# HGRN2 score matmuls reordered by shape over the chunks, and the meta state padded to 128 rows

## Chip, cores and metric

One core of a Trainium2 chip runs the whole program. The metric is the device time of one execution in microseconds (us); the median of three timed runs stands for the kernel before. The engines are named as in the profile: PE is TensorE (matmuls), PEld its weight loads, DVE VectorE, ACT ScalarE, POOL GpSimd, SP the engine that only issues DMAs here.

## The reference, cut to what matters

A decoder block reads 512 tokens with 16 learned meta tokens ahead of them. It mixes tokens with forgetting attention and with an HGRN2 recurrence, and ends in a mixture of experts. The change touches the recurrence, which for 8 heads (key and value width 128) computes, chunk by chunk:

```
b = cumsum(log_f); o_inter = (q * exp(b)) @ state
scores[t, s] = sum_k q[t, k] * k[s, k] * exp(b[t, k] - b[s, k])   for s <= t
o = o_inter + scores @ v
new_state = exp(b_last) * state + (k * exp(b_last - b)).T @ v
```

The first chunk is the 16 meta tokens; it only provides the first state.

## The kernel before

The program has two halves. In the first, a list of projections (`proj`, line 344 through `mm3`) runs on PE: 128-column tiles of the input weights, each split by ACT (line 158) and DVE (line 159, `cut`) into a high and a low part, are multiplied with the normalised input. Beside them `stage` holds a generator per HGRN head (`hgrn`) and per attention pair (`attend`); after every three matmuls of a projection `stage.step()` lets the generator issue its next piece, so the pieces of a head stand between the projections of the next head in PE's order. A scheduler of the language orders the instructions of these engines; SP's DMAs are in the order of the code. In the second half 201 MB of expert weights (`w_e`, tile `ch`) stream in while PE multiplies them (lines 1126 and 1166). Tiles of the stream live in slots that the first half's tiles give free.

`hgrn` takes the 512 tokens of a head as 4 chunks of 128. The score matrix of a chunk is built from squares below the diagonal, each from factors that are referred to the middle of the square (`levels`): one 64x64 square (`l64`, called the far pair), two 32x32 squares (`l32`), and in the four 32x32 diagonal blocks one matmul of 32 columns (`kys`, `qys`) and three of 16 columns (`l4`, `l8`, `l16`). All contract over 128 rows. Far pairs and `l32` squares go to the PSUM tile `pc` (view `p4`), the diagonal blocks to `pd` (view `d4`). The output rows of a matmul are the PSUM partitions that it writes, and so its column group of the array: 64 wide for the far pair, 32 wide for all others. In the code that the diff shows, the loop over chunks `c` is outermost and the four matmuls of a diagonal block stand together.

DVE then masks `pd` into `sD` (lines 564 and 566), ACT copies `pc` into the score tile `sT` (lines 569 to 571), and the diagonal blocks follow (lines 575 and 577). Four steps after the score matmuls PE multiplies the scores with the values (tile `po`, lines 582 and 583).

The meta state: `pm` holds the transposed values and keys of the 16 meta tokens, line 510 copies them to `mt_`, a tile of 16 partitions, and line 519 multiplies them over 16 rows into `pi`, ahead of the three state updates of line 521, which contract over 128 rows.

In the early part, lines 222 to 225 (`fa`) project the forget gates: 8 matmuls per token block with 32 output rows each, the inner loop over the four column groups.

Of the kernel before, what the change touches and what calls it, by code (L numbers as in the profile page):

```python
# [13 lines left out]
AF = mybir.ActivationFunctionType  # L14
# [4 lines left out]
M = 16  # L19
# [4 lines left out]
NB = S // 128  # L24
# [40 lines left out]
def hybrid_block(tc, I, out, dbg=None):  # L65
    nc = tc.nc
    V, A, G, T = nc.vector, nc.scalar, nc.gpsimd, nc.tensor
    ctx = ExitStack()
    with ctx:
# [8 lines left out]
        def slot(name, n=4, dt=F32, w=None, stream=False):  # L78

            t_ = sb.tile([128, SLOT], dt, tag="stream" if stream else "slot", bufs=STREAM if stream else SLOTS, name=name)  # L80
            w = w or {4: L, 2: 1024, 1: 2048}[n]
            return t_[:, :n * w].rearrange("p (n w) -> p n w", n=n)
# [5 lines left out]
        def bank(name, main=False):  # L88
            return ps.tile([128, 512], F32, tag="main" if main else "side", bufs=4, name=name)
# [11 lines left out]
        ca, cc = slot("ca", 1)[:, 0], slot("cc", 1)[:, 0]  # L101
        used = {}

        def inside(c, n, dt=F32):

            o = used.get(id(c), 0)
            used[id(c)] = o + n
            return c[:, o:o + n].bitcast(dt)
# [306 lines left out]
            V.memset(sT[i], 0.0)  # L415
            V.memset(sD[i], 0.0)

        mt_ = inside(cc, 256)[:M]

        LEV = (64, 32, 16, 8, 4)  # L420

# [34 lines left out]
        def hgrn(h, f, b, q, v, g, kd, qe):  # L456
# [5 lines left out]
            def by(ap, w):  # L462
                return ap.rearrange("p (c t) -> p c t", t=w)
# [42 lines left out]
            pm = bank("pm")  # L506
            T.transpose(pm[:M, 0:128], v[:, 0:M], ident)
            T.transpose(pm[:M, 128:256], kd[:, 0:M], ident)
            mt = mt_[:, 0:256]
            V.tensor_copy(mt, pm[:M, :256])  # L510
            A.activation(eb[:, 3], br, AF.Exp)
            for _ in range(2):
                yield
# [21 lines left out]
            for j, w in enumerate(LEV):  # L535
                e = by(lev[j], 2 * w)
# [11 lines left out]
            p4, d4 = by(pc, 128), by(pd, 128)  # L548
            l64, l32, l16, l8, l4 = lev
            for c in range(NB):  # L550
                o = 128 * c
                T.matmul(p4[0:64, c, 64:128], l64[:, o:o + 64], l64[:, o + 64:o + 128], start=True, stop=True)
                for j in range(2):
                    r = slice(64 * j, 64 * j + 32)
                    T.matmul(p4[r, c, 64 * j + 32:64 * j + 64], l32[:, o + 64 * j:o + 64 * j + 32],
                             l32[:, o + 64 * j + 32:o + 64 * j + 64], start=True, stop=True)
                for j in range(4):
                    r, o = slice(32 * j, 32 * j + 32), 128 * c + 32 * j
                    T.matmul(d4[r, c, 0:32], kys[:, o:o + 32], qys[:, o:o + 32], start=True, stop=True)
                    for z_, (l, w) in enumerate(((l4, 4), (l8, 8), (l16, 16))):  # L560
                        T.matmul(d4[r, c, 32 + 16 * z_:48 + 16 * z_], l[:, o:o + 32],  # L561
                                 by(l[:, o:o + 32], 2 * w)[:, :, w:], start=True, stop=True)
            sc, sd = sT[h % 2], sD[h % 2]
            V.copy_predicated(sd, m4c, d4[:, :, 0:32])
            for z_, w in enumerate((4, 8, 16)):
                V.copy_predicated(sd.rearrange("p c (a t) -> p c a t", t=2 * w)[:, :, :, w:],
                                  mx_[w].rearrange("p c (a t) -> p c a t", t=w),
                                  d4[:, :, 32 + 16 * z_:48 + 16 * z_].rearrange("p c (a t) -> p c a t", t=w))
            A.activation(sc[0:64, :, 64:128], p4[0:64, :, 64:128], AF.Copy)
            A.activation(sc[0:32, :, 32:64], p4[0:32, :, 32:64], AF.Copy)  # L570
            A.activation(sc[64:96, :, 96:128], p4[64:96, :, 96:128], AF.Copy)
            for j in range(4):
                r = slice(32 * j, 32 * j + 32)
# [28 lines left out]
        for h in range(8):  # L602
            pf = proj(True)
            f, v, b, kd = (piece(n_, keep=n_ in "fv") for n_ in ("f", "v", "b", "kd"))
            q, g, qe = (piece(n_, F32, S) for n_ in ("q", "g", "qe"))
            logistic(f, pf, True)
            pi = proj(True)
            if h == 0:
                m4c, mx_ = within()
            both(lambda o, i_: A.activation(o, i_, AF.Copy), v, pi)  # L610
            V.tensor_scalar(f, f, lb[:, 1, h:h + 1], lb[:, 0, h:h + 1], op0=ALU.mult, op1=ALU.add)
            A.activation(b, f, AF.Ln)
            V.tensor_tensor_scan(b, reset, b, 0.0, op0=ALU.mult, op1=ALU.add)
            V.tensor_scalar(f, f, -1.0, 1.0, op0=ALU.mult, op1=ALU.add)
            pq = proj(False)
            A.activation(q, pq, AF.Copy, scale=128 ** -0.5)
            pg = proj(False)
            logistic(g, [pg], later=True)
            stage.add(hgrn(h, f, b, q, v, g, kd, qe))
# [10 lines left out]
        for d in range(KD):  # L630
            wh, wl = weights()
            p = bank("py", True)
# [6 lines left out]
        def attend(pr, X, Y, v):  # L639
# [7 lines left out]
            yield  # L647
            pm = bank("pm")
            T.transpose(pm[:M, 0:128], v[:, 0:M], ident)
            vm = mt_[:, 128 * (pr % 2):128 * (pr % 2) + 128]  # L650
            V.tensor_copy(vm, pm[:M, :128])
            yield
            hd = [slice(64 * h, 64 * h + 64) for h in range(2)]
# [18 lines left out]
            for i in range(NB):  # L672
                P = M + 128 * i
                r = slice(128 * i, 128 * i + 128)
# [35 lines left out]
            for c in range(NB):  # L710
                for h in range(2):
                    T.matmul(po[hd[h], 128 * c:], vt[:, c, hd[h]], pt_[h][:, 512 * c:384 * c + 512],  # L712
                             start=(c == 0), stop=(c == NB - 1))
# [8 lines left out]
        for pr in range(4):  # L722
            pk = proj(True)

            Y = slot("Y", 4, F32R)
            X = [[piece(f"X{h}{j}", F32R, S) for j in range(2)] for h in range(2)]
            for h in range(2):
                r = slice(64 * h, 64 * h + 64)
                nc.gpsimd.dma_start(Y[64:66, 2 * h + 1], chl[2 * pr + h:2 * pr + h + 1])
                V.tensor_scalar(X[h][1][64:66], mhalf[64:66, 0:1].to_broadcast([2, S]), 2.0, None, op0=ALU.mult)  # L730
                both(lambda o, i_: A.activation(o, i_[r], AF.Copy), Y[0:64, 2 * h], pk)
                for i in range(2):
                    o = slice(264 * i, 264 * i + 264)
                    V.tensor_tensor(Y[0:64, 2 * h + 1, o], pk[i][r], Y[0:64, 2 * h, o].bitcast(F32), op=ALU.subtract)
                G.tensor_copy(Y[64:128, 2 * h], Y[0:64, 2 * h].bitcast(F32))
            pq = proj(False)
            for h in range(2):
                r = slice(64 * h, 64 * h + 64)
                A.activation(X[h][0][0:64], pq[r], AF.Copy, scale=0.125)
                V.scalar_tensor_tensor(X[h][0][64:128], pq[r], 0.125, X[h][0][0:64].bitcast(F32), op0=ALU.mult, op1=ALU.subtract)  # L740
                G.tensor_copy(X[h][1][0:64], X[h][0][0:64].bitcast(F32))
            pv_ = proj(True)
            v_ = piece("v")
            both(lambda o, i_: A.activation(o, i_, AF.Copy), v_, pv_)
            stage.add(attend(pr, X, Y, v_))
# [11 lines left out]
        for d in range(KD):  # L757
            wh, wl = weights()
            p = bank("py", True)
            mm3([p], wh, wl, lambda k, i: oaT_h[:, k], lambda k, i: oaT_l[:, k], 4)  # L760
            g, t = ga[d], mix[d // 4][:, d % 4]
# [491 lines left out]
        with tc.If(nc.values_load(extrai[0:1, 32:33], min_val=0, max_val=16) > 0):  # L1253
# [4 lines left out]
            for half in range(2):  # L1258
                with tc.For_i(0, 16) as p:
# [4 lines left out]
                    with tc.For_i(0, nb):  # L1264
# [19 lines left out]
                        for k in range(KD):  # L1284
                            w = slot("wx", 2)[:, 0]
                            nc.sync.dma_start(w, I["w_e"][bass.ds(12 * p + k, 1), :, 1024 * half:1024 * half + 1024]
                                              .rearrange("o p c -> (o p) c"))
                            for n in range(2):
                                T.matmul(ph[n], xT[k // 4][:, k % 4], w[:, 512 * n:512 * n + 512],
                                         start=(k == 0), stop=(k == KD - 1))  # L1290
# [7 lines left out]
                        for n in range(2):  # L1298
                            for k in range(4):
                                w = slot("wx", 2)[:, 0, :512]  # L1300
                                c = 1024 * (k % 2) + 512 * half
# [4 lines left out]
                        for n in range(2):  # L1306
                            A.activation(yh, py[n], AF.Copy)
                            V.tensor_tensor(yl, py[n], yh.bitcast(F32), op=ALU.subtract)
                            c = slice(512 * n, 512 * n + 512)
# [66 lines left out]
```

## Time and profile before

| | |
|---|---|
| timed runs | 1098.28 us median of 3 (1097.28 to 1099.87) |
| the profiled execution | 1096.76 us, of which its span is 1094.8 us |
| busy in the span | PE 1047.2 us (96%), PEld 689.2, DVE 575.0 (53%), ACT 329.5 (30%), POOL 67.7 |
| mean granted clock of PE | 0.993 |
| w_e stream | 189 transfers of 1024 KB, DMA engines at 420 GB/s from about 700 us on |

The profile covers one execution. The span is from its first to its last instruction; a row of the timeline begins with the start in us from the span's start and the duration in us. A matmul in fp32 is one instruction of the program and two records each of weight load and matmul in the trace; records overlap, so that the distance of starts, not the duration, tells what one costs. Idle time in brackets is that of the engine before the row, and what ended it.

### The profile page before, as it was taken

The numbers are of one execution on the slowest core, as the hardware profiler recorded it, in microseconds if no ns is written. First come the engines' busy times: TensorE is split into PE (matmuls) and PEld (weight loads), VectorE is DVE, ScalarE is ACT, GpSimd is POOL, SyncE is SP. The second block draws the span as 40 slices with busy tenths as digits, with TensorE's granted clock in tenths as the row PEclk, the third lists the DMA queues.
The fourth block names the chain that finished last, engine by engine and source line by source line (L and its number), as shares of the span: only waits on it lengthen the run. The fifth ranks groups of instructions, "written<-read, shape, count | busy, mean of one in ns | idle before, by whom it ended". The sixth has DMA issues, their size and how long they took to land.

```text
span 1094.8 us, 16543 instructions
## 1 busy us (share of the span) xinstructions
PE 1047.2 (96%) x6756; PEld 689.2 (63%) x6757; DVE 575.0 (53%) x1269; ACT 329.5 (30%) x643; POOL 67.7 (6%) x88
## 2 busy tenths in 40 slices
PE   9999999999999999999999999999999999988984
PEld 8888988988888898777788634333443333333331
DVE  6967877677633466666653533333443333323324
ACT  5545655555551243344434300000000000000003
POOL 5000000000000121100000000000000000000002
PEclk9999999999999999999999999999999999999997
DMA  6211221121222211221287999999999999999993
GB/s 221 95 44 74 78 78 43 75 79 40 78 86 89 96 59 59 79 77 39 77 323 299 321 419 419 418 419 420 419 418 420 419 419 420 420 420 418 420 415 127
DMA packets 41139, 255.61 MB, mean 233 GB/s; under 512 B 6143, under 2 KB 6399, under 8 KB 12000
## 3 DMA queue, kind: packets, MB, share of 16 engines
q1 hardware_dynamic: 37328, 248.39, 57.3%
q0 software_dynamic: 2416, 3.98, 1.0%
q10 hardware_dynamic: 1312, 2.11, 0.5%
q8 instruction: 55, 0.90, 0.3%
q14 instruction: 28, 0.23, 0.1%
HBM read 254.15 MB, written 4.19 MB: 236 GB/s over the span
## 4 chain that ended last, share of the span: by engine, by line
PE 60%; DMA 32%; DVE 4%; issue 1%; ACT 1%; POOL 0%; DVEq 0%; SPq 0%; ACTq 0%; POOLq 0%
DMA ch<-w_e 30%; PE pj L344 24%; PE py L344 6%; PE pk L344 5%; PE phu L1126 4%; PE pye L1166 4%; PE pd L561 1%; PE ph L1026 1%; PE pu L215 1%; PE ph L1024 1%; PE poa L712 1%; PE ph L1025 1%; PE pout L1212 1%; DMA xslot<-rows_of,xslot 1%; DMA rows_of<-v 1%
## 5 line engine op out<-in xcount | busy, mean ns | idle before, releaser
L344 PE MATMUL pj<-uh,ws 128*128 128x512 f32 (+1 forms) x928 | 295.0, 363 | 1.6 <-DVE ws L159 1.1
L1126 PE MATMUL phu<-ch,xslot 128*64 128x512 f32 x1024 | 232.6, 598 | 20.7 <-DMA ch<-w_e 20.7
L344 PEld LDWEIGHTS pj<-uh,ws 128*128 128x128 f32 x928 | 174.8, 189 | 27.3 <-issue 2.0
L1126 PEld LDWEIGHTS phu<-ch,xslot 128*64 128x64 f32 x1024 | 68.1, 136 | 175.9 <-issue 113.0
L344 PE MATMUL pj<-ul,ws 128*128 128x512 f32 (+1 forms) x464 | 164.1, 354 | 0.0
L1139 DVE TENSOR_TENSOR hs<-hs,phu 128x512 f32<-128x512 f32 x16 | 11.0, 688 | 208.6 <-PE phu L1126 191.4
L159 DVE TENSOR_TENSOR ws<-w,ws 128x1024 fp32r<-128x1024 f32 (+1 forms) x84 | 98.0, 1168 | 34.3 <-ACT ws L158 34.1
L1166 PE MATMUL pye<-ch,hs 128*64 128x512 f32 x512 | 113.9, 596 | 1.6 <-DVE hs L1152 1.1
L158 ACT ACTIVATE ws<-w 128x1024 fp32r<-128x1024 f32 (+1 forms) x83 | 84.2, 1015 | 54.0 <-PE py L344 40.3
L344 PE MATMUL pk<-uh,ws 128*128 128x264 f32 x352 | 95.4, 285 | 0.0
L344 PEld LDWEIGHTS pj<-ul,ws 128*128 128x128 f32 x464 | 87.4, 188 | 9.5 <-issue 0.2
L1214 DVE SCALAR_TENSOR_TENSOR x<-pout,gate,x 128x512 f32<-128x512 f32 x128 | 87.1, 742 | 1.1 <-PE pout L1213 1.1
L1138 ACT ACTIVATE hs<-phu 128x512 f32<-128x512 f32 x16 | 9.6, 597 | 254.6 <-PE phu L1126 254.6
L1166 PEld LDWEIGHTS pye<-ch,hs 128*64 128x64 f32 x512 | 35.1, 137 | 71.5 <-issue 64.6
L1170 ACT ACTIVATE yh<-pye 128x512 fp32r<-128x512 f32 x32 | 19.1, 598 | 163.2 <-PE pye L1166 163.2
L344 PEld LDWEIGHTS pk<-uh,ws 128*128 128x128 f32 x352 | 66.4, 189 | 0.6
L1171 DVE TENSOR_TENSOR yl<-pye,yh 128x512 fp32r<-128x512 f32 x32 | 22.1, 692 | 70.3 <-ACT yh L1170 68.7
L1212 PE MATMUL pout<-yh,PT 128*128 128x512 f32 x128 | 57.0, 445 | 0.0
L1213 PE MATMUL pout<-yl,PT 128*128 128x512 f32 x128 | 50.5, 395 | 0.2 <-DVE yl L1171 0.2
L344 PE MATMUL pk<-ul,ws 128*128 128x264 f32 x176 | 50.0, 284 | 0.0
L1212 PEld LDWEIGHTS pout<-yh,PT 128*128 128x128 f32 x128 | 24.0, 187 | 27.4 <-issue 13.8
L344 PE MATMUL py<-ohh,ws 128*128 128x512 f32 x128 | 40.3, 394 | 0.0
(323 smaller groups left out, 1520.7 us busy)
## 6 DMA issues: line engine op xcount, KB each, us to landing
ch<-w_e SPq DMA_DIRECT2D x189, 1024.0 KB, 20.0
w<-w_h SPq DMA_DIRECT2D x16, 1024.0 KB, 5.1
w<-w_gh SPq DMA_DIRECT2D x4, 1024.0 KB, 4.9
w<-w_ho SPq DMA_DIRECT2D x4, 1024.0 KB, 4.9
w<-w_a SPq DMA_DIRECT2D x4, 1024.0 KB, 5.0
w<-w_ga SPq DMA_DIRECT2D x4, 1024.0 KB, 4.9
w<-w_o SPq DMA_DIRECT2D x4, 1024.0 KB, 4.8
x<-x SPq DMA_DIRECT2D x4, 512.0 KB, 5.2
```

Source lines behind the costliest of these rows:

```text
L158: a = A.activation(wh, w, AF.Copy)
L159: b = V.tensor_tensor(wl, w, wh.bitcast(F32), op=ALU.subtract)
L215: T.matmul(pvs[b, i][:, k], rows[b][1][:, 512 * i + 128 * k:512 * i + 128 * k + 128], dgs[b], start=True, stop=True)
L344: T.matmul(p[i], a[:, k], m(k, i), start=(k == 0 and j == 0), stop=(k == nk - 1 and j == 2))
L1126: T.matmul(ph[n][r], x_[k // 4][:, k % 4, r], w[2 * e + n], start=(k == 0), stop=(k == KD - 1))
L1139: V.tensor_tensor(hs, hs, ph[1], op=ALU.mult)
L1166: T.matmul(py[n][r], hs[:, 128 * k + 64 * e:128 * k + 64 * e + 64], w[2 * (k % 2) + e], start=(k == 0), stop=(k == 3))
L1170: A.activation(yh[n], py[n], AF.Copy)
L1171: V.tensor_tensor(yl[n], py[n], yh[n].bitcast(F32), op=ALU.subtract)
L1212: T.matmul(po, PT[:, tb], yh[n], start=True, stop=False)
L1213: T.matmul(po, PT[:, tb], yl[n], start=False, stop=True)
L1214: V.scalar_tensor_tensor(x[tb][:, c], po, gate[:, tb, p:p + 1], x[tb][:, c], op0=ALU.mult, op1=ALU.add)
```

## The change

In `hgrn` the loop over chunks moves inside: first the four far pairs, then the eight `l32` squares, then the 16 `kys` matmuls, then the 48 of `l4`, `l8` and `l16`, each with the column group as the innermost loop. The far pairs of chunks 1 and 3 are written to partitions 64 to 127 of `pc`, into columns 0 to 63 of their chunk, which nothing else uses; they are copied by an ACT instruction of their own to the place in the score tile where they were before. `mt_` has 128 partitions, is cleared once, and line 519 (521 in the new file) contracts over 128 rows.

```diff
-        mt_ = inside(cc, 256)[:M]
+        mt_ = inside(cc, 256)
+        V.memset(mt_, 0.0)
...
-            V.tensor_copy(mt, pm[:M, :256])
+            V.tensor_copy(mt[:M], pm[:M, :256])
...
             for c in range(NB):
                 o = 128 * c
-                T.matmul(p4[0:64, c, 64:128], l64[:, o:o + 64], l64[:, o + 64:o + 128], start=True, stop=True)
+                far = p4[64:128, c, 0:64] if c % 2 else p4[0:64, c, 64:128]
+                T.matmul(far, l64[:, o:o + 64], l64[:, o + 64:o + 128], start=True, stop=True)
+            for c in range(NB):
+                o = 128 * c
                 for j in range(2):
                     r = slice(64 * j, 64 * j + 32)
                     T.matmul(p4[r, c, 64 * j + 32:64 * j + 64], l32[:, o + 64 * j:o + 64 * j + 32],
                              l32[:, o + 64 * j + 32:o + 64 * j + 64], start=True, stop=True)
+            for c in range(NB):
                 for j in range(4):
                     r, o = slice(32 * j, 32 * j + 32), 128 * c + 32 * j
                     T.matmul(d4[r, c, 0:32], kys[:, o:o + 32], qys[:, o:o + 32], start=True, stop=True)
-                    for z_, (l, w) in enumerate(((l4, 4), (l8, 8), (l16, 16))):
+            for z_, (l, w) in enumerate(((l4, 4), (l8, 8), (l16, 16))):
+                for c in range(NB):
+                    for j in range(4):
+                        r, o = slice(32 * j, 32 * j + 32), 128 * c + 32 * j
                         T.matmul(d4[r, c, 32 + 16 * z_:48 + 16 * z_], l[:, o:o + 32],
                                  by(l[:, o:o + 32], 2 * w)[:, :, w:], start=True, stop=True)
...
-            A.activation(sc[0:64, :, 64:128], p4[0:64, :, 64:128], AF.Copy)
+            p5, s5 = (z_.rearrange("p (c e) t -> p c e t", e=2) for z_ in (p4, sc))
+            A.activation(s5[0:64, :, 0, 64:128], p5[0:64, :, 0, 64:128], AF.Copy)
+            A.activation(s5[0:64, :, 1, 64:128], p5[64:128, :, 1, 0:64], AF.Copy)
...
-            vm = mt_[:, 128 * (pr % 2):128 * (pr % 2) + 128]
+            vm = mt_[:M, 128 * (pr % 2):128 * (pr % 2) + 128]
```

On PE, in the score matmuls of the first head, the kernel before has these rows for the first chunk (the last three rows come four times in a chunk, for the four diagonal blocks, and the whole four times in a head):

```order
L552 MATMUL pc<-ea 64x64
L555 MATMUL pc<-ea 32x32 x2
L559 MATMUL pd<-eb 32x32
L561 MATMUL pd<-fs 32x16
L561 MATMUL pd<-ea 32x16 x2
```

The changed kernel has at the same place, for all four chunks of the head (its line numbers are 3 to 11 higher; the first and the last row are projections):

```order
L344 MATMUL pj<-uh_92,ws 128x512
L555 MATMUL pc<-ea 64x64 x4
L560 MATMUL pc<-ea 32x32 x8
L565 MATMUL pd<-eb 32x32 x16
L570 MATMUL pd<-fs 32x16 x16
L570 MATMUL pd<-ea 32x16 x32
L344 MATMUL pj<-uh_92,ws 128x512
```

The same 76 matmuls stand in another order, the four 64-wide ones together; where the blocks stand among the projections is the same in all eight heads.

On DVE, in the setup of the first head (`cc` and `fz` are gate tiles, `f` the first head's forget gates, `ws` a split weight tile), the kernel before has:

```order
L404 TENSOR_TENSOR cc<-cc 128x8
L365 TENSOR_SCALAR f<-f 128x528
L390 SCALAR_TENSOR_TENSOR fz<-fz 8x528
L405 RECIPROCAL cc<-cc 128x8
L391 SCALAR_TENSOR_TENSOR fz<-zero_307,fz 8x528
L406 TENSOR_TENSOR cc<-cc 128x8
L159 TENSOR_TENSOR ws<-w,ws 128x1024
L393 CAST cc<-fz 8x528
L407 TENSOR_SCALAR cc<-cc 128x8
```

The changed kernel has there:

```order
L404 TENSOR_TENSOR cc<-cc 128x8
L420 MEMSET cc 128x256
L390 SCALAR_TENSOR_TENSOR fz<-fz 8x528
L405 RECIPROCAL cc<-cc 128x8
L391 SCALAR_TENSOR_TENSOR fz<-zero_307,fz 8x528
L406 TENSOR_TENSOR cc<-cc 128x8
L365 TENSOR_SCALAR f<-f 128x528
L393 CAST cc<-fz 8x528
L407 TENSOR_SCALAR cc<-cc 128x8
L159 TENSOR_TENSOR ws<-w,ws 128x1024
```

The clearing of `mt_` is new, line 365 moves behind the scan of line 391, and the split of a weight tile (line 159) moves behind lines 393 and 407.

## Rows read from the trace of the kernel before

**Rows 1.** The page: its head, and the chain that ended last, by engine.
```profile
span 1094.8 us, 16543 instructions
...
PE 60%; DMA 32%; DVE 4%; issue 1%; ACT 1%; POOL 0%; DVEq 0%; SPq 0%; ACTq 0%; POOLq 0%
```

**Rows 2.** Busy time by stretch: PE, PEld, DVE, ACT, POOL, PE clock, DMA share, GB/s.
```profile
55.00:300.00 245.00, 244.48 (x2525) 217.31 (x2524) 178.81 (x390) 130.29 (x239) 9.13 (x10) 1.00 0.19 66
...
700.00:1000.00 300.00, 284.51 (x1334) 107.52 (x1332) 110.77 (x194) 17.92 (x30) 9.89 (x10) 1.00 1.01 420
```

**Rows 3.** Waits of PE: us in total, times, longest.
```profile
PE pj L344 <- DVE ws L159: 1.1, 1, 1.1
```

**Rows 4.** Waits of SP's DMA queue: us in total, times, longest.
```profile
SPq L144 <- DVE ws L159: 473.7, 35, 19.7
```

**Rows 5.** Timeline of PE, score matmuls of the first head.
```profile
61.75 0.33 PE L552 MATMUL pc<-ea 128*64 128x64 f32 x2
...
62.68 0.28 PE L561 MATMUL pd<-ea 128*32 128x16 f32 x4
62.88 0.33 PE L552 MATMUL pc<-ea 128*64 128x64 f32 x2
63.14 0.26 PE L555 MATMUL pc<-ea 128*32 128x32 f32 x4
...
66.30 0.51 PE L344 MATMUL pj<-uh,ws 128*128 128x512 f32 x1
```

**Rows 6.** Records of tiles `pd` and `pc`: duration in ns (min/median/max).
```profile
L561 PE MATMUL pd<-ea x512: 182/183/183, 62.2 to 291.0; 128*32 128x16 f32 x171
...
L552 PE MATMUL pc<-ea x64: 222/246/270, 61.7 to 290.1; 128*64 128x64 f32 x64
```

**Rows 7.** Timeline of PEld: first loads of two neighbouring diagonal blocks.
```profile
62.38 0.14 PEld L559 LDWEIGHTS pd<-eb 128*32 128x32 f32 x2
...
62.53 0.14 PEld L559 LDWEIGHTS pd<-eb 128*32 128x32 f32 x2
```

**Rows 8.** Timeline of PE: line 225 (`fa`) for the 16 meta tokens.
```profile
10.91 0.32 PE L225 MATMUL pf<-u,wfa 128*32 128x16 f32 x16
```

**Rows 9.** Line 225: duration of its records in ns (min/median/max).
```profile
L225 PE MATMUL pf<-u,wfa x80: 182/273/298, 10.9 to 19.8; 128*32 128x128 f32 x64, 128*32 128x16 f32 x16
```

**Rows 10.** Timeline of PE around the meta state of the second head.
```profile
84.45 0.28 PE L344 MATMUL pk<-uh,ws 128*128 128x264 f32 x1
84.66 0.48 PE L519 MATMUL pi<-cc 16*128 16x128 f32 x2
85.07 0.94 PE L521 MATMUL pi<-fs,ca 128*128 128x128 f32 x6
85.77 0.37 PE L344 MATMUL pj<-uh,ws 128*128 128x264 f32 x1
```

**Rows 11.** Timeline of PE: scores times values, second head.
```profile
101.26 0.38 PE L582 MATMUL po<-fs,ca 128*128 128x128 f32 x2
101.48 0.39 PE L583 MATMUL po<-fs,qe 128*128 128x128 f32 x2
```

**Rows 12.** Timeline of DVE in the setup.
```profile
32.13 1.21 DVE L159 TENSOR_TENSOR ws<-w,ws 128x1024 fp32r<-128x1024 f32 x1
33.26 0.42 DVE L393 CAST cc<-fz 8x528 fp32r<-8x528 f32 x1
33.61 0.15 DVE L407 TENSOR_SCALAR cc<-cc 128x8 f32<-128x8 f32 x1
```

**Rows 13.** Groups of instructions on DVE: busy us, mean ns of one, idle before.
```profile
L415 DVE MEMSET ca<- 128x512 f32 x2 | 1.0, 485 | 0.1
```

**Rows 14.** Timelines of DVE and ACT: score tiles of the second head.
```profile
98.46 0.30 DVE L564 COPY_PREDICATED ca<-ca,pd 128x128 f32<-128x128 int32 x1 [1.86 <-PE pd L561]
...
99.88 0.63 ACT L575 ACTIVATE ca<-ca 32x128 f32<-32x128 f32 x2 [0.64 <-DVE ca L566]
```

**Rows 15.** Line 564: what DVE waited for ahead of it, us in all, times.
```profile
  PE pd L561: 21.0, 8
```

## Prediction

> **What bounds the kernel now.** I read the page first: the chain that ended last is 60% PE and 32% DMA [rows 1], so there are two bounds, one after the other. The table of busy time by stretch says where. From 55 to 300 us, where the eight HGRN heads run, PE is busy 244.48 of 245 us at a granted clock of 1.00, DVE 178.81 of them. From 700 to 1000 us the DMA engines are full at 420 GB/s [rows 2], which is the stream of expert weights. The list of PE's waits has next to nothing in the first half: the projections wait 1.1 us, once, for a split weight tile [rows 3]. So until the stream takes over, time taken out of PE's queue is time taken out of the kernel, if the stream then starts earlier too. SP's waits say that it does: its queue of weight loads waits 473.7 us in all for split tiles to be used up [rows 4], and the expert weights stand behind them in the same queue and need slots that the first half gives free. Nothing in the second half hangs on a fixed time.
>
> **The score matmuls, now.** The timeline shows the first head's block from 61.75 to the next projection at 66.30: 4.55 us, four chunks of 1.13 [rows 5]. Three distances in it matter. (1) Within one column group the records stand 0.03 apart: the last four of a chunk take 0.28, less the 0.18 of the last one [rows 5, 6], so 0.10 for three steps. (2) Neighbouring diagonal blocks, 8 records in one group each, start 0.15 apart [rows 7], 0.019 a record: a group starts while the one before still works, so two overlap, no more. (3) Going to the 64-wide matmul and back costs a pause: from the last 32-wide record, at 62.68 + 0.10, to 62.88 is 0.10 in place of 0.03, and the far pair holds PE from 62.88 to 63.14, 0.26 for two records [rows 5], though a second one in the same group would add only 0.33 less 0.22, so 0.11 [rows 5, 6].
>
> **The same with the new order.** Four far pairs, two in each half: 0.26 + 0.11 = 0.37, if the halves overlap. Behind them groups 0 and 2 have four `l32` squares and sixteen diagonal matmuls each, 20 matmuls or 40 records; groups 1 and 3 have 32. If all four groups step on their own, 39 steps of 0.032 are 1.25. With 0.10 to the next projection and 0.03 for the shift between groups the block is 1.75 us: 2.8 saved, 22.4 in eight heads.
>
> That four groups can do this, the block itself can't show. One other place does: the forget-gate projection of the meta tokens has the same 32-wide, 16-column form with the groups innermost, and its 16 records end in 0.32 with 0.18 for the last [rows 8, 9]: 15 starts in 0.14, 0.009 each, which is 0.035 for a round of four. So the step within a group stays as it is with all four at work, and they write one PSUM tile together. It is a burst of only 8 matmuls. Whether PE can be fed at that rate, 0.018 a matmul, through 72 of them is the open price: the slowest reading is rows 7, four matmuls in 0.15 or 0.038 each, with which the block is 0.37 + 72 x 0.038 + 0.13 = 3.2, and the saving 1.3 a head, 10.6 in all. I take the burst, as it is the row of the same order and shape, and keep 10.6 as the lower end.
>
> [...]
>
> **The meta state.** Line 519 over 16 rows stands between matmuls over 128 rows. From the projection at 84.45 to the one at 85.77 PE spends 1.32 [rows 10] on nine records. Records of 128 columns without such a change stand 0.11 apart (two from 101.26 to 101.48) [rows 11]; nine of these are 0.99. Padded to 128 rows, line 519 needs no pause ahead of it or behind: 0.33 a head, 2.6 in all. The least is nothing, the most 0.4 a head, were the first load hidden wholly.
>
> **What is added.** DVE clears 256 columns once; 512 cost 0.485 [rows 13], so between nothing and 0.49. More is moved: the split of the third weight tile, for which PE already waits [rows 3], went at 32.13, ahead of lines 393 and 407, and now goes behind these two and line 365. 393 takes 0.35 until 407 starts [rows 12], 365 (528 columns too) I take as the same, 407 as 0.1: 0.8 later, and all of it falls on PE. With the clearing exposed too it is 1.3. The far pairs' copy becomes two ACT instructions in place of one; two copies of 32 rows take 0.63 [rows 14], so the extra one is some 0.3. It is hidden, since `pc` is now complete about 1 us ahead of `pd`, and nobody needs it before `po`; without that cover it would be 2.4.
>
> **What is late next.** DVE waits 1.86 us for `pd` in the second head [rows 14], 21.0 in all eight [rows 15]. With `pd` ready 2.8 earlier it comes 0.94 late there. The score tile is then complete at 99.88 + 0.63 = 100.51, in old times, plus 0.94; PE wants it a load (0.11) ahead of 101.26 [rows 11, 14]. The margin of 0.64 doesn't hold: a wait of 0.3. If five heads are like this, the other three have (21.0 - 9.3) / 3 = 3.9 and are not late. 5 x 0.3 = 1.5.
>
> **Sum.** 22.4 + 2.6 - 0.8 - 1.5 = 22.7 us less. The profiled execution took 1096.76, 1.96 of it outside its span, and 1.5 less than the median; from it the result is 1074.1, from the median 1098.28 it is 1075.6. I predict 1075.
>
> **Rivals.**
> - The four groups don't keep up: PE is fed more slowly than in the burst, or only pairs overlap as now. For: no row shows more than 16 records at that pace. Against: the 0.019 of rows 7 follows from the order now, where a group's eight records keep the next group out until they are nearly done. Then DVE is not late (1.3 is under 1.86): 10.6 + 2.6 - 0.8 = 12.4, 1086. Between the two paces it is 1078 to 1086. [...]
> - [...]
> - DVE's chain takes over: it cannot come earlier in the five heads at all, and PE waits the whole 0.94 and the same again before the next pieces. 9.4 in place of 1.5: 1083.5. Against: DVE's 178.81 us in 245 are 80% of the 222 that would be left.
> - Slower: the score tile comes so late that PE loses at `po` all that it won. The place is line 582; the price is the lateness of DVE and ACT less the margin of 0.64. It decides from (22.4 + 2.6 - 0.8) / 8 = 3.0 us a head on. For that the evictions would have to double (98.46 to 100.51 is 2.05 now) and more, and only an ACT copy from partitions 64 to 127 into 0 to 63 is new in them, which no row here shows. At 3.5 a head it is 1102.
>
> **Chances.** My forecast (1072 to 1078) 0.55, the groups not keeping up 0.27, DVE's chain 0.09, loads in a row 0.04, no measurable change for another reason 0.02, slower 0.03. About 0.2% (2.2 us) is what a measurement of this kernel can tell from no change: faster by more 0.94, within it 0.03, slower 0.03. The range takes 1071 (nothing lost at `po`, the meta state at 0.4 a head, the split less late) to 1086, where the groups keep today's pace.
>
> **What would show it.** Right: a block of about 1.75 us in every head, its last four records of one round about 0.01 apart, no 64-wide matmul between 32-wide ones; line 521 with 0.11 between records and no gap; the wait of line 344 for a split tile near 1.9; small waits at `po`; the stream starting some 23 us earlier at the same 420 GB/s. Wrong: records 0.02 or more apart inside the block (first rival), PE waits for DVE or ACT of more than 2 us in all at `po` (third and fourth), or a block shorter as said and a stream that starts no earlier.

## The result: 1082.1 us, and the profile after

The changed kernel took 1082.08 us (median of 4 runs, 1080.37 to 1084.21) against 1097.98 for the kernel before beside it: a ratio of 0.9859, interval [0.9847, 0.9871], so 15.9 us less. The prediction was 1075 in a range of 1071 to 1086. The time fell as foretold, but by seven tenths of the 22.7 us that the sum had, and most of what is missing has a place.

The page's head, and the busy time by stretch (columns as in [rows 2]), for the profiled execution of 1081.51 us:

```profile
span 1079.7 us, 16553 instructions
```
```profile
55.00:300.00 245.00, 240.55 (x2599) 212.76 (x2598) 184.96 (x400) 141.38 (x261) 9.36 (x10) 0.99 0.21 71
700.00:1000.00 300.00, 284.04 (x1324) 107.61 (x1324) 114.43 (x201) 19.13 (x32) 10.76 (x11) 1.00 1.01 419
```

The stream at the end runs as before, 419 GB/s. In the stretch of the heads PE, idle for 0.5 of 245 us before, now stands for 4.4, and its mean clock is 0.99. The waits of PE and of SP's queue (us in total, times, longest) say for what, `px` being behind the heads:

```profile
PE pj L344 <- issue: 3.4, 1, 3.4
PE pj L344 <- DVE ws L159: 1.7, 1, 1.7
PE px L1019 <- DMA xslot<-rows_of,xslot: 1.6, 1, 1.6
PE po L593 <- ACT ca L586: 1.1, 4, 0.3
```
```profile
SPq L144 <- DVE ws L159: 457.2, 35, 21.3
```

SP's wait for splits is 16.5 us shorter than in [rows 4], and its first load of expert weights is issued as much earlier (timeline of SP's queue, before and after):

```profile
555.76 3.58 SPq L928 DMA_DIRECT2D ch<-w_e  x7
...
539.25 4.75 SPq L939 DMA_DIRECT2D ch<-w_e  x8
```

So what PE wins in the heads does reach the stream. The score block itself is what was hoped for. PE's timeline, first head:

```profile
61.84 0.45 PE L555 MATMUL pc<-ea 128*64 128x64 f32 x8
62.22 0.41 PE L560 MATMUL pc<-ea 128*32 128x32 f32 x13
...
62.49 0.45 PE L565 MATMUL pd<-eb 128*32 128x32 f32 x30
62.75 0.44 PE L570 MATMUL pd<-fs 128*32 128x16 f32 x30
...
63.05 0.70 PE L570 MATMUL pd<-ea 128*32 128x16 f32 x62
63.68 0.50 PE L344 MATMUL pj<-uh,ws 128*128 128x512 f32 x1
```

From 61.84 to the next projection at 63.68 are 1.85 us (1847 or 1848 ns in all eight heads), where [rows 5] has 4.55. The 62 records of the last row start within 0.70 - 0.18 = 0.52, so 0.0085 apart: the pace of the short burst of [rows 8], kept up through the block. The meta state (compare [rows 10]):

```profile
81.83 0.28 PE L344 MATMUL pk<-uh,ws 128*128 128x264 f32 x1
81.95 0.38 PE L521 MATMUL pi<-cc 128*128 128x128 f32 x2
82.17 0.83 PE L523 MATMUL pi<-fs,ca 128*128 128x128 f32 x6
82.76 0.37 PE L344 MATMUL pj<-uh,ws 128*128 128x264 f32 x1
```

From 81.83 to 82.76 are 0.93 us in place of 1.32: 0.39 a head. And the waits of DVE for `pd`, 21.0 us in eight heads in [rows 15], are nearly gone, so DVE now comes late:

```profile
  PE pd L570: 2.6, 3
```

**Where the third went.** Heads without a new wait now follow one another in 29.0 us, against 32.06 to 32.13: 3.09 less, as block and meta state say (2.70 + 0.39). Distances are from the start of one head's score block to the next. From the fourth to the fifth it is 34.97, and there the timeline shows (idle time and its end in brackets):

```profile
152.38 0.62 PE L344 MATMUL pj<-uh,ws 128*128 128x512 f32 x2
152.84 0.39 PE L344 MATMUL pj<-ul,ws 128*128 128x512 f32 x1
156.61 1.01 PE L344 MATMUL pj<-uh,ws 128*128 128x512 f32 x2 [3.37 <-issue]
157.42 0.63 PE L344 MATMUL pj<-ul,ws 128*128 128x512 f32 x1
```

PE stands for 3.37 us with nothing in the profile that it waits for, which is what "issue" means, and then works at about half pace: from the start of the two matmuls at 156.61 to the next are 0.81 us, where two took 152.84 - 152.38 = 0.46 ahead of the pause. Busy time in pieces of 2 us (PE, PEld, DVE, ACT, POOL, PE clock, DMA share, GB/s):

```profile
150.00:152.00 2.00, 2.00 (x154) 1.90 (x154) 1.97 (x4) 0.97 (x4) 0.00 (x0) 1.00 0.59 106
152.00:154.00 2.00, 1.23 (x5) 0.86 (x5) 0.92 (x4) 0.95 (x3) 0.00 (x0) 1.00 0.98 414
154.00:156.00 2.00, 0.00 (x0) 0.00 (x0) 0.83 (x4) 0.61 (x2) 0.00 (x0) 0.77 0.05 16
156.00:158.00 2.00, 1.39 (x4) 1.10 (x4) 0.00 (x0) 0.00 (x0) 0.00 (x0) 0.50 0.03 8
158.00:160.00 2.00, 2.00 (x8) 1.61 (x7) 0.42 (x1) 1.47 (x2) 0.00 (x0) 0.50 0.00 0
160.00:162.00 2.00, 2.00 (x11) 2.00 (x11) 1.23 (x1) 0.19 (x1) 0.00 (x0) 0.53 0.00 0
162.00:164.00 2.00, 2.00 (x13) 1.74 (x12) 0.69 (x1) 0.60 (x1) 0.00 (x0) 1.00 0.00 0
```

The granted clock is at 0.50 from 155.1 to 161.9; PE works from 156.61 on, so half of the 5.3 us left, some 2.6 as an estimate, is lost there. Just ahead of the pause stands the densest stretch of the head (154 matmul records in 2 us) and, over its end, a 1 MB weight load that fills the DMA engines (share 0.98 from 152 to 154 us). The DMA view of the pause, first up to 154.3 us and then from there (queue, kind: packets, MB, share), has in the first window only the load, and in the second a packet of PE's own instructions:

```profile
q1 hardware_dynamic: 143, 1.05, 83.2%
...
q8 instruction: 1, 0.02, 4.6%
```

The page's table of queues has 55 packets and 0.90 MB of `q8` in all, so 16 KB each; that it is PE's program is read from its counts, 13,513 records of PE and PEld, some 246 a packet. A score block is 304 records: more than one packet, and now used up in 1.85 us.

The trace also shows that this packet is late. Packets of `q8` that meet no load start at even distances in PE's program: the 3rd, 4th, 9th, 11th and 17th when 656, 910, 2194, 2700 and 4236 records have started, so 256 a packet. The 12th, at 154.42, starts at record 3242, some 280 records behind that distance, which PE had reached about 4 us before, at 150.44, near the load's start at 150.79.

### The profile page after: what moved, and what is told of

Its sections match the earlier page's. It is cut to its first block, busy times and chain, and to the rows that moved or that the text cites. A ratio compares the mean times of both kernels' runs of the same rounds, so it can differ in the third digit from the quotient of the medians.

```text
span 1079.7 us, 16553 instructions
## 1 busy us (share of the span) xinstructions
PE 1026.8 (95%) x6756; PEld 670.8 (62%) x6757; DVE 574.7 (53%) x1270; ACT 331.8 (31%) x651; POOL 67.8 (6%) x88
## 4 chain that ended last, share of the span: by engine, by line
```

## Experiments

**Theory A**: the pause is a fetch of PE instructions that falls due in the dense block of the fourth head, while a weight load stands in front of it in the DMA engines. **Theory B**: the block is too dense whatever stands where in the program, or it is a thing of that moment. The first two runs move PE's program against its fetches (fetch: the transfer of one such packet), by matmuls of one column in a place where PE waits for a split tile anyway (64 here, 16 in pages_eighth); nothing reads what they write.

```diff
             p = bank("pj", True)
+            [T.matmul(p[32 * (i % 4):32 * (i % 4) + 32, 0:1], onesb[:, 32 * (i % 4):32 * (i % 4) + 32],
+                      onesb[:, 0:1], start=True, stop=True) for i in range(64 if state["n"] == 3 else 0)]
             mm3([p], wh, wl, lambda k, i: uh[k // 4][:, k % 4, M:], ...
```

**pages_half.** 

> The changed kernel with 64 one-column matmuls (128 PE instructions, half a 256-instruction fetch) put ahead of the third projection, where PE waits 1.7 us for a split tile anyway; everything behind them stands half a fetch later in PE's program. Theory A (the pause of 3.4 us in the fourth head's block, and the lower clock behind it, come from a fetch of PE instructions that falls due in the dense block while a 1 MB weight load fills the DMA engines): the fetches fall due elsewhere, no head has an 'issue' wait of more than about 1.2 us, the granted clock stays at 1.00 from 55 to 300 us, and the time is 5 us less, near 1077. Theory B (the block itself is fed too fast in that head, whatever stands where in the program, or the pause is a thing of that moment, as a throttle): the pause and the clock stay in the fourth head, 1082.

Measured: 1077.39 us (1075.72 to 1078.76), ratio 0.9816 [0.9799, 0.9832]: 4.7 less than the changed kernel. The fourth head takes 29.57 us, and no 'issue' wait is left in the heads but one of 0.25, in the third: it ends at 128.47, 2.3 us behind a fetch that started at 126.16, again near the end of a load (122.83 to 126.39). So a late fetch is still there, but costs only the 0.25 us in this place. In this profile the clock is also at the lower level from 34.5 to 37.9, behind the added matmuls; best1 and best1_again have the same matmuls and no such stretch. Busy time by stretch, clock third from the end:

```profile
55.00:300.00 245.00, 243.56 (x2628) 215.20 (x2628) 187.40 (x404) 145.09 (x268) 9.34 (x10) 1.00 0.22 74
```

**pages_eighth.** 

> The same with 16 one-column matmuls, 32 PE instructions. Theory A, with the fetches of the changed kernel moved 32 instructions earlier against its weight loads: the fetch of the fourth head falls due before its block and its pause goes; that of the seventh head, near 240 us, now falls due inside its block with a load in front of it, and PE stands 3 to 4.5 us there, with the half clock behind it. The time stays at 1081 to 1083, but the place moves three heads on. Theory B: the pause stays in the fourth head, near 153 us.

Measured: 1079.05 (1077.01 to 1082.99), 0.9838 [0.9811, 0.9866]. The fourth head takes 29.58 us, and the pause is in the seventh head. PE's timeline, then the DMA view up to 244.3 us and from there:

```profile
243.55 0.40 PE L344 MATMUL pj<-ul,ws 128*128 128x512 f32 x1
246.75 0.73 PE L344 MATMUL pj<-uh,ws 128*128 128x512 f32 x2 [2.81 <-issue]
```
```profile
q1 hardware_dynamic: 141, 1.05, 78.8%
...
q8 instruction: 1, 0.02, 4.6%
```

The head was foretold by A from the places of fetches and loads alone, and B is out. The pause is a little shorter than foretold (3 to 4.5). Here the clock stayed at 1.00 behind it, so only the pause is lost, and the median came out 2 us below the 1081 to 1083 expected.

**half_loads** is the other half of A's claim: the place of the fetches stays, the load in front of them is shorter.

```diff
-            want(I["w_h"][2 * h], 2048, [0, 1024])
-            want(I["w_h"][2 * h + 1], 2048, [0, 1024])
+            for j in range(4):
+                want(I["w_h"][2 * h + j // 2][:, 1024 * (j % 2):1024 * (j % 2) + 1024], 1024, [0])
```

> The changed kernel with each 1 MB load of the HGRN heads' weights made as two loads of 512 KB, each fetched when its half is due; PE's program and with it the place of its instruction fetches stay as they are. Theory A (a fetch of PE instructions waits for the load in front of it): a load now takes about 1.8 us in place of 3.6, so a fetch that falls due in a block is at most that late; the pause of 3.4 us in the fourth head becomes 1.6 or less, the half clock behind it goes (with a pause of 2.8 us it did not fall), and the time is 3.5 to 5.3 us less than the changed kernel's 1082, so 1077 to 1079. Theory C (the fetch is late by itself, and load and pause only fall together because both hang on the same step of the program): the pause stays at 3.4 us and the time at 1082, or worse, as small loads may come later for their splits.

Measured: 1075.55 (1074.40 to 1075.86), 0.9800 [0.9784, 0.9817]. The pause, in the fourth head as before, is

```profile
155.93 0.62 PE L344 MATMUL pj<-uh,ws 128*128 128x512 f32 x2 [2.29 <-issue]
```

1.08 us shorter than 3.37. The load took about 2.5 us and not the 1.8 that I had (from 151.2 to 153.7, in place of 3.6 from 150.8 to 154.4; the block starts 0.41 later here), so it ended 1.1 us earlier against the block, and the pause shrank by that. The size was missed, the mechanism held, and Theory C of the expectation (the fetch is late by itself) is out. PE goes on at the same distance behind the start of the packet in the changed kernel, pages_eighth and half_loads: 154.42 to 156.61, 244.38 to 246.75, 153.73 to 155.93, so 2.2 to 2.4 us. In every other run with an 'issue' wait in the heads, it is 2.3 to 2.5. The last head's block starts 3.1 us earlier than in the changed kernel. The other 3.4 came behind the heads, which A doesn't explain; 1.3 of it in the profile is a shorter wait for a row gather (`px`, 0.3 for 1.6), and best2 below bears on the rest.

**order_only** and **pad_only** take the change apart. order_only leaves the meta state as it was before.

```diff
 order_only: the new loops, but
-                far = p4[64:128, c, 0:64] if c % 2 else p4[0:64, c, 64:128]
-                T.matmul(far, l64[:, o:o + 64], ...
+                T.matmul(p4[0:64, c, 64:128], l64[:, o:o + 64], ...
 pad_only: only mt_ = inside(cc, 256), its memset, and [:M] where 16 rows are meant
```

> The kernel before with the new order of the scores alone: no padding of the meta state, no second half for the far pairs (all four write the lower half, one copy takes them out). By the terms of the sum: the four far pairs stand 0.11 us apart in two groups, 0.26 + 0.33 = 0.59 in place of 0.38, so the block is about 2.05 us; 2.5 us a head less than before, 20 in all; no gain of the meta state (3.1), no later split at the start (0.7). If the pause of the fourth head stays (theory A: its place in the program is the same, so about 3 us and 2 us of lower clock): 1098 - 20 + 5 (pause) + 2 (waits at po) = 1085. If the pause needs the padding or the halves: 1080.

Measured: 1081.39 (1080.14 to 1081.95), 0.9851 [0.9834, 0.9867]: not to be told from the whole change. The block is 2.08 us, the far pairs 0.61 of it:

```profile
63.20 0.68 PE L552 MATMUL pc<-ea 128*64 128x64 f32 x8
63.81 0.41 PE L557 MATMUL pc<-ea 128*32 128x32 f32 x13
```

So the second half is worth 0.23 a head. The pause is there, 3.0 us, with 3.4 us of lower clock. What I had wrong is the waits at `po`: this kernel's list has none, so they come only with the halves and the padding. These two win 0.23 + 0.39 a head, 5.0 us in all. Of that the waits at `po` take 2.4, the later split 0.6, and a longer pause and lower clock 1.2 (34.97 for 34.42 in heads that are 0.62 shorter).

> The kernel before with the meta state padded to 128 rows and nothing else. By the sum's two terms as the changed kernel's trace has them: 0.39 us a head less at the meta state, 3.1 in all, and the third weight tile's split later by 0.6 to 0.7 us at the start, so 2.4 us less than before: 1095. The pause of 0.5 us in the fourth head stays. If the padded matmul only moves its gap (to the transposes ahead of it), 1098.

Measured: 1094.91 (10 runs, 1094.28 to 1097.61), 0.9978 [0.9968, 0.9988], 2.9 us less than before, where 2.4 was expected. Heads follow in 31.73 us (0.34 to 0.40 less). The pause in the fourth head is 0.8 and not 0.5, and PE's wait for the split is 1.7 in place of 1.1:

```profile
PE pj L344 <- DVE ws L159: 1.7, 1, 1.7
```

**groups_apart** keeps the shapes together but puts a column group's four chunks next to each other.

```diff
-            for c in range(NB):
-                for j in range(4):
+            for j in range(4):
+                for c in range(NB):        # the same for l32 and for l4, l8, l16
                     r, o = slice(32 * j, 32 * j + 32), 128 * c + 32 * j
```

> The changed kernel, by shape as it is, but with the four chunks of one column group next to each other, so that a group's records follow one another and neighbours seldom stand in different groups. Theory 1 (the gain is that four column groups work at once): as rows 7 of the kernel before, 0.15 us for a diagonal block of four matmuls, 72 x 0.038 + 0.38 + 0.13 = 3.2 us a block, 1.35 a head more than now, 10.8 in all; the denser pause shrinks by about 1.4; 1091. Theory 2 (the gain is that shapes no longer alternate, and the order of groups doesn't matter): a block of 1.85 us as now, 1082.

Measured: 1086.87 (1084.97 to 1089.36), 0.9899 [0.9882, 0.9915]. The block is 3.34 us, 1.49 more than with the groups innermost. The last 61 records of PE's timeline show the pace:

```profile
65.50 1.38 PE L570 MATMUL pd<-ea 128*32 128x16 f32 x61
66.81 0.50 PE L344 MATMUL pj<-uh,ws 128*128 128x512 f32 x1
```

(1.38 - 0.18) / 60 = 0.020 apart, the 0.019 of [rows 7], and not 0.0085. Theory 1 holds: more than half of the gain is that four column groups work at once. Of the 2.70 us that the block won, 1.49 go with the order of the groups and the rest, 1.21, with shapes and halves (0.23 of it the halves, by order_only). The time rose by 4.8 and not by 8 x 1.49 = 11.9. In part that is shown: the pause is 2.0 us here and the lower clock lasts 3.4 us (the fourth head loses 3.8 in place of 5.97), and no wait at `po` is left (2.4). From the first block to the last this kernel takes 5.9 us more than the changed one, and 7 x 1.49 - 2.2 - 2.4 is 5.8.

**po_later** puts the score times value matmuls one piece of the projection later.

```diff
-            for _ in range(4):
+            for _ in range(5):
                 yield
             po = bank("po")
```

> The changed kernel with the score times value matmuls (po) one piece of the projection later: five yields in place of four, 24 to 50 columns x 512 more of PE's work in front of them, about 0.7 us. If the waits at po are DVE and ACT coming some tenths late in about five heads, as the sum had it, the waits go, and the time is 2.4 us less than the changed kernel's, near 1079.7, with the pause in the fourth head as it was. If what is late moves on (the transposes behind po wait in their turn, or the next head's pieces), the waits stand at pt and nothing is won: 1082.

Measured: 1078.92 (1077.86 to 1079.55), 0.9827 [0.9810, 0.9843], 3.2 less. No wait at `po` or `pt` stands in the list of the heads, and the heads that took 29.55 now take 29.01. The pause of 3.4 is there; the lower clock behind it lasted 3.4 us in place of 6.8, so the fourth head takes 33.89 in place of 34.97, and that is the part of the gain that was not expected.

**best1** joins the 64 matmuls, the later `po`, and the clearing of `mt_` put behind the first head's masks (`m4c, mx_ = within(); V.memset(mt_, 0.0)`). 

> The changed kernel with three edits: the 64 one-column matmuls that move PE's instruction fetches by half a fetch, po one piece later, and the clearing of the meta state's tile behind the first head's masks, so that the third weight tile's split comes first. By theory A, and if the waits at po go: 1077.4 of the first edit alone, less 2.4, less up to 0.7: 1074 to 1075, with a granted clock of 1.00 through the heads and no 'issue' wait over 1 us. If the later po shifts the loads into another block, a pause of 1 to 3 us comes back: 1077.

Measured: 1071.35 (1071.19 to 1074.32), 0.9770 [0.9751, 0.9789]. That is 3 us less than expected. PE stands for only 0.3 us in the heads, 0.23 of it an 'issue' wait in the third (columns as above):

```profile
55.00:300.00 245.00, 244.74 (x2629) 216.97 (x2629) 184.82 (x400) 145.75 (x267) 9.35 (x10) 1.00 0.22 74
```

> The same kernel as best1 once more, as the measure for best2 beside it: 1071 to 1073.

 Measured for best1_again: 1073.92 (5 runs, 1071.66 to 1075.95), 0.9785 [0.9768, 0.9801], a little above what was expected. The two medians are 26.5 and 23.4 us below the kernel before beside them, and the sum's two gains alone, 22.4 + 2.6, are 25.0.

**best2**: 

> best1 with the weights of the HGRN heads loaded in halves of 512 KB. In best1 no pause and no lower clock is left for a shorter load to take away, and the loads of half_loads won 3.1 us in the heads (all of it pause and clock) but 6.5 in all. If the other 3.4 us came from what the halved loads themselves do behind the heads, they come here again: 1068. If they came from where the streams happened to start, nothing is won: 1071 to 1073. A fetch that now falls due behind another half load could bring a pause of up to 2.3 us back: 1074.

Measured: 1072.60 (1068.54 to 1073.88), 0.9773 [0.9753, 0.9792], not to be told from best1_again. No gain of the halved loads' own is seen; the profiled executions of best1_again and best2 drift 5 us apart in the stream alone, between 780 and 940 us by PE's matmuls, with the same instructions there. So the 3.4 us of half_loads behind its heads are most likely of that kind, but this was not shown.

## Why the prediction was right in direction and 7 us short

Its terms, in us against before, with what the traces have:

| step of the sum | predicted | measured |
|---|---|---|
| score block, 8 heads | -22.4 | -21.6 (2.70 a head) |
| meta state, 8 heads | -2.6 | -3.1 (0.39) |
| split of the third weight tile | +0.8 | +0.6 (wait 1.7 for 1.1) |
| waits at `po` | +1.5 | +2.4 (four heads 0.5 to 0.8 longer) |
| pause and lower clock, fourth head | not in the sum | +5.2 |
| sum | -22.7 | -16.5; by the medians -15.9, by the profiled executions -15.3 |

That the time lies in the stated range of 1071 to 1086 is in part luck. The range reaches above 1078 for groups that don't keep up and for DVE's chain, and neither happened: 1082 came from a pause that no rival has.

- **The block.** The likeliest case was right: the burst of [rows 8] is the pace of the whole block, 1.85 for 1.75, with records 0.0085 apart where the sum had 0.008 (0.032 for a round of four). The slow reading from [rows 7], a block of 3.2, describes the order of groups_apart (3.34). No run shows loads in a row (chance 0.04): 144 records at the 0.03 that [rows 5] have within a group would be 4.3 us a block, an estimate, and it took 1.85 here and 3.34 in groups_apart.
- **The meta state.** The step was right and sized low: 0.39 a head came, where the sum had 0.33 and its upper bound, for a first load hidden wholly, was 0.4.
- **The start.** Right: DVE's clearing is put ahead of the split, and the wait of line 344 rose from 1.1 to 1.7; pad_only shows the same 1.7, order_only, without the clearing, 1.1.
- **What is late next.** The place was right, line 593 of the changed kernel, and so was that DVE and ACT come some tenths late. The term was too small: four heads wait 0.24 to 0.30 each, and each costs 0.5 to 0.8. That the difference is the first weight load after the pause, no longer hidden, is argued, not shown. po_later took both away.
- **The step that went wrong** is in the part on bounds: "time taken out of PE's queue is time taken out of the kernel". It held in seven heads. In the fourth, PE stood in an 'issue' wait of 3.37 us, by Theory A because it was out of instructions, and 5.2 us of the gain went. The kernel before had a pause at the same place of the program, at 163.98 us, with a fetch that started at 162.1, at the end of a load from 158.5; it ended at 164.50. Its list of PE's waits has it, and I had left it out of rows and sum as a trifle:

```profile
PE pj L344 <- issue: 0.5, 1, 0.5
```

 By Theory A a block that is used up in 1.85 us and not in 4.55 brings PE to the end of its instructions earlier, while the packet still starts at the load's end (154.42 here, 162.1 before). That the cause of the pause is the fetch behind the load rests on three runs that pull in different directions: moved by half a packet it is down to 0.25 us and in the third head, moved by an eighth it is in the head foretold, and with a load that ends 1.1 us earlier it is shorter by the same 1.1 us.
- **DVE's chain and the slower case**, the third and the fourth rival, did not occur: 2.4 us at `po` in all, where 9.4 and 24 would have been needed.

The fourth head's 34.97 are 5.97 over the 29.0 of an undisturbed one, and the kernel before already lost 0.74 there (32.81 for 32.07), so 5.2 net. Of the 5.97, 3.4 are the pause, and the other 2.6 are what the half clock costs by its length, 5.3 us of work. In po_later the same two terms give 3.4 + 1.5 = 4.9, and its fourth head is 4.88 over the others. The changed kernel's later row gather (`px`, 1.6 us for 0.4) cost another 1.2 in its profile; the other kernels have between no wait and 2.4 (pages_half) there, so I take it for scatter. With it the sum is -15.3, as the profiled executions have it.

## What to carry to other kernels

When small matmuls are packed closer, look at who feeds PE with instructions: count its records per fetched packet (about 256 here), find the fetches that fall due in the dense stretch (here 154 matmul records in 2 us), and see which bulk load stands ahead of them. An unexplained 'issue' wait of half a microsecond in the trace before is the place to look, since here it grew as the code around it got faster (0.5, 0.8 in pad_only, 3.4), and moving the code took almost all of it away (0.25 in pages_half). The small matmuls here, which write 32 partitions each, took 1.85 us a block when they went round the four column groups and 3.34 when they stayed in one. Not all that the edit won was kept, since the engines that empty PSUM lost their slack: 2.4 us went in waits at `po`, and one piece more ahead of `po` took them away.

## What the runs showed of the hardware that was not expected

- Four column groups at work start a record every 0.0085 us over 62 records (changed kernel); with a group's records next to each other it is 0.020 (groups_apart).
- Packets of PE instructions (16 KB) start about 256 records apart where no load is under way (254 from the 3rd to the 4th in the changed kernel). One that falls due during a 1 MB load mostly starts at the load's end: from 55 to 330 us of the changed kernel's trace twelve packets start during a load, eleven of them in its last 0.6 us (one at 154.42, the load from 150.79 to 154.42). Not always: there one started at 93.16, in a load from 92.83 to 97.04, and in the kernel before one at 97.56, in the middle of a load from 95.44 to 99.91. Behind an 'issue' wait in the heads PE goes on 2.2 to 2.5 us after the packet's start, in the traces of ten kernels and in the third, fourth or seventh head.
- The granted clock does not follow the length of PE's pause alone: behind 3.4 us it was at 0.50 for 6.8 us (changed kernel) and at a lower level for 3.4 (po_later), behind 3.0 (order_only) and 2.0 (groups_apart) for 3.4 each, and behind 2.8 (pages_eighth) and 2.3 (half_loads) it did not fall. In groups_apart it fell only 1.3 us after PE had gone on, and in pages_half at 34.5 us behind a wait of 1.1. What decides between them stays open.
